# q turned as plain head pairs, q and k-v tiles in turn, and low parts of weights moved, in the projection of a hybrid encoder layer

## The chip, the cores and the metric

The kernel runs on one core of a Trainium2 chip. The metric is the device time of one execution in microseconds. TensorE (PE) multiplies and transposes, VectorE (DVE) and ScalarE (ACT) work element by element, GpSimd (POOL) does so more slowly, and SyncE (SP) issues the DMAs. Each engine works through its own list of instructions in order and waits on semaphores for what other engines make. PE writes into PSUM; DVE and ACT read it from there.

## The reference

One encoder layer over 1024 tokens of width 1024: a feed-forward half step, then attention and a state-space scan side by side on one input projection, an output projection, a second feed-forward half step and an embedding gate, each with a layer norm. What the change touches is the projection and what is done with q and k:

```python
u = x @ w_in[i]
q, k, v, z, xs, bm, cm, dt_raw = jnp.split(u, SPLIT_POINTS, axis=-1)
qf = _rms(q.reshape(B, S, N_Q_HEADS, HEAD_DIM), q_norm[i])
kf = _rms(k.reshape(B, S, N_KV_HEADS, HEAD_DIM), k_norm[i])
qh = _apply_rope(qf, cos, sin)
kh = _apply_rope(kf, cos, sin)
...
xbc = jnp.concatenate([xs, bm, cm], axis=-1)     # then a convolution over the tokens
```

There are 8 q heads and 2 k-v heads of 64.

## The kernel before

Everything is float32, and accuracy is kept by splitting each operand into a high part (rounded to the format that PE multiplies fast, made by a copy on ACT) and a low part (the rest, a subtraction `lo` on DVE, L87). `mm3` then makes three products for one: high by low, low by high, high by high (L122).

Tokens are cut into 8 tiles of 128. The stage in question is `qkv_part`. It stands between the products for z (with the layer norm of tokens 4 to 7 and their transposes, L224, beside them) and the eight tiles x0 to x7 of `xbc_part`, each of two halves of 512 tokens; a convolution over each x tile follows on ACT and DVE.

In `qkv_part` all eight q tiles (`qq`, 24 products of 128x512) come first, then all eight k-v tiles (`kv`, 24 products of 128x272). After each tile, `step` does three things with a lag. `norm` squares the tile on ACT (L865), sums it per head on DVE (L867) and takes the power -1/2 on GpSimd (L870). `rope` refines that with a Newton step and turns the pairs of q or k by the tables (L877 to L890). Then a `turn` transposes the result on PE: that of q transposes, for each of 8 heads, the 64 high and 64 low columns as one 128x128 block into a big PSUM buffer (L929), and ACT copies the 128x1024 result into Q (L930). To have them, q is split beforehand (a copy, L923, and a subtraction into `qs`). That of k transposes two blocks (L911) into a small buffer, and K's high and low parts are made from there (L913 and L87).

`step` takes one turn off the list `late` when more than `keep` wait there. The last turns are put on `self.pend` and taken by `pop`, two at a time, after each half of x0 (`xbc_gemm`). So x0's halves are each followed by two k turns.

PSUM has 2 big buffers of 128x1024 and 4 small ones of 128x512. x tiles use the big ones, and hold them until their convolution has read them.

Weights come by DMA into `raw` buffers, are cast by ACT into a ring of 10 blocks (L108), and their low parts are made by DVE. The k-v weights are loaded while the last two q tiles run (`kv_weights`), those of the x tiles (`wx`) when `xbc_weights` is called. A scheduler orders each engine's list by the order of the code and its dependences; `issue_after` and `behind` hold an instruction back behind a marked one.

Of the kernel before, what the change touches and what calls it, by code (L numbers as in the profile page):

```python
# [18 lines left out]
P = 128  # L19
# [17 lines left out]
class Layer:  # L37
# [771 lines left out]
        self.nc.sync.dma_start(out=t, in_=self.I[key].broadcast_to([P, n]))  # L809
        return t  # L810

    def kv_weights(self, part):
        if part == 0:
            self.wkv = []
        for k in ((0,), (3, 6))[part]:
            n = min(3, KD - k)
            r = self.raw(self.I["wkv"][:, k * 272:(k + n) * 272], n * 272)
            self.wkv += [self.split(r[:, i * 272:(i + 1) * 272], 272) for i in range(n)]
# [22 lines left out]
    def qkv_part(self, c, xT):  # L841
        nc, tc, I = self.nc, self.tc, self.I
        Q, K, V = self.qkv
        tabs = c.enter_context(tc.tile_pool(name="tabs", bufs=1))
        wk = c.enter_context(tc.tile_pool(name="qwork", bufs=2))
        cs = tabs.tile([P, NT, HD], F32, name="cs")
        sn = tabs.tile([P, NT, HD], F32, name="sn")
        nc.sync.dma_start(out=cs, in_=I["cs"])
        nc.sync.dma_start(out=sn, in_=I["sn"])
        dtb = self.bcast(tabs, "dtb", "dt_bias", 16)  # L850
        T = {}

        def tables(nm, scale):
            w = self.bcast(tabs, f"w_{nm}", f"{nm}n", HD)
            ws = self.bcast(tabs, f"ws_{nm}", f"{nm}ns", HD)
            T1 = tabs.tile([P, NT, HD], F32, name="T1")
            T2 = tabs.tile([P, NT, HD], F32, name="T2")
            for t_, a, b in ((T1, cs, w), (T2, sn, ws)):
                nc.vector.scalar_tensor_tensor(out=t_, in0=a, scalar=scale, in1=b.unsqueeze(1).broadcast_to([P, NT, HD]), op0=ALU.mult, op1=ALU.mult)
            T[nm] = (T1, T2)  # L860

        def norm(ps, nh):
            v = ps.rearrange("p (h d) -> p h d", d=HD)
            sq = wk.tile([P, nh, HD], F32, name="sq")
            nc.scalar.activation(out=sq, in_=v, func=AF.Square)  # L865
            ss = self.small.tile([P, 16], F32, name="ss")[:, :nh]
            nc.vector.reduce_sum(ss, sq, axis=AX.X)  # L867
            nc.vector.tensor_scalar(out=ss, in0=ss, scalar1=1.0 / HD, scalar2=RMS_EPS, op0=ALU.mult, op1=ALU.add)
            r = self.small.tile([P, 16], F32, name="qr")[:, :nh]
            nc.gpsimd.tensor_tensor(out=r, in0=ss, in1=self.mhalf[:, :nh], op=ALU.pow)  # L870
            return v, nh, sq, ss, r

        def rope(v, nh, m, ss, r, nm, t):

            self.newton(r, ss, nh)
            qn = wk.tile([P, nh, HD], F32, name="qn")
            nc.vector.tensor_tensor(out=qn, in0=v, in1=r.unsqueeze(2).broadcast_to([P, nh, HD]), op=ALU.mult)  # L877
            T1, T2 = (x[:, t] for x in T[nm])
            H2 = HD // 2
            for a in range(2):  # L880
                o = slice(a * H2, (a + 1) * H2)
                i = slice((1 - a) * H2, (2 - a) * H2)
                nc.vector.tensor_tensor(out=m[:, :, o], in0=qn[:, :, i], in1=T2[:, o].unsqueeze(1).broadcast_to([P, nh, H2]), op=ALU.mult)
            nc.vector.tensor_tensor(out=qn, in0=qn, in1=T1.unsqueeze(1).broadcast_to([P, nh, HD]), op=ALU.mult)
            if nm == "q":
                nc.vector.tensor_tensor(out=qn, in0=qn, in1=m, op=ALU.add)
                return qn
            kn = wk.tile([P, NKV, 2, HD], F32, name="kn", bufs=4)
            a, b = (x.unsqueeze(2).broadcast_to([P, NKV, 2, HD]) for x in (qn, m))
            nc.vector.tensor_tensor(out=kn, in0=a, in1=b, op=ALU.add)  # L890
            return kn

        NK = NKV * HD
        late = []

        def kv_front(t, ps):
            nc.vector.tensor_tensor(out=self.dt[:, t], in0=ps[:, 256:272], in1=dtb, op=ALU.add)
            vv = ps[:, NK:2 * NK].rearrange("p (g d) -> p g d", d=HD)
            st = norm(ps[:, :NK], NKV)
            nc.scalar.copy(out=V[:, t, :, 0], in_=vv)  # L900
            self.lo(V[:, t, :, 1], vv, V[:, t, :, 0])
            return st

        def kv_back(t, st):

            kn = rope(*st, "k", t)

            def turn():
                pt = self.pss()[:, :NKV * P].rearrange("p (g t) -> p g t", g=NKV)
                for g in range(NKV):  # L910
                    nc.tensor.transpose(out=pt[:, g], in_=kn[:, g].rearrange("p a d -> p (a d)"), identity=self.ident)  # L911
                hi, lo = (K[:, :, j, t * P:(t + 1) * P] for j in range(2))
                nc.scalar.copy(out=hi, in_=pt)  # L913
                self.lo(lo, pt, hi)
            late.append(turn)

        def q_front(t, ps):
            return norm(ps, NQ)

        def q_back(t, st):  # L920
            qs = wk.tile([P, NQ, 2, HD], F32R, name="qs", bufs=4)
            qn = rope(*st, "q", t)
            nc.scalar.copy(out=qs[:, :, 0], in_=qn)  # L923

            def turn():
                pt = self.psb().rearrange("p (h t) -> p h t", t=P)
                qv = qs.bitcast(F32)
                for hh in range(NQ):
                    nc.tensor.transpose(out=pt[:, hh], in_=qv[:, hh].rearrange("p a d -> p (a d)"), identity=self.ident)  # L929
                nc.scalar.copy(out=Q[:, :, t * P:(t + 1) * P], in_=pt)  # L930
            late.append(turn)
            return qs[:, :, 1], qn, qs[:, :, 0]

        backs, los = [], []

        def step(t, ps, front, back, keep=1):


            if len(late) > keep or not front:
                late.pop(0)()  # L940
            st = front(t, ps) if front else None
            if los:
                self.lo(*los.pop())
            if backs and (todo := backs.pop()()):
                los.append(todo)
            if front:
                backs.append(lambda: back(t, st))

        tables("q", HD ** -0.5)
        for t in range(NT):  # L950
            ps = self.qq(t, xT)
            if t >= NT - 2:
                self.kv_weights(t - NT + 2)
            step(t, ps, q_front, q_back)
        for t in range(NT):
            ps = self.kv(t, xT)
            step(t, ps, kv_front, kv_back, 2)
            if t == 0:
                tables("k", 1.0)
        self.pend += [lambda: step(NT, None, None, None)] * 4  # L960
        self.x0 = self.xbc_gemm(0, xT, 1)
        assert not late and not backs and not los

    def xbc_weights(self, j):
        return [b.rearrange("p l (k c) -> p l k c", c=P) for b in self.wload(self.I["wx"][j])]

    def xbc_half(self, w, xT, h, ps):
        self.mm3(ps, [((w[k // 4][:, 0, k % 4], w[k // 4][:, 1, k % 4]), tuple(x[:, k % 4] for x in xT[h][k // 4])) for k in range(KD)])
# [1 line left out]
    def xbc_gemm(self, j, xT, n):  # L970

        w = self.xbc_weights(j)
        ps = self.psb()
        for h in range(2):
            self.xbc_half(w, xT, h, ps[:, h * 512:(h + 1) * 512])
            if n == 1 or n and h:
                self.pop(2)
        return ps

    def xbc_part(self, c, wk, xT, prep):  # L980
# [18 lines left out]
        for j in range(8):  # L999
            a = wk.tile([P, S], F32, name="conv", bufs=3)  # L1000
            if j < 7:
                ps = self.x0 if j == 0 else self.xbc_gemm(j, xT, 2 if j > 1 else 0)
                conv(j, a, ps, 0, S, 0, S, True)
                nc.scalar.activation(out=a, in_=a, func=AF.Silu)
            else:
                w = self.xbc_weights(j)
                self.wz = [b for k in range(4) for b in self.wload(I["wz"][k])]
                p0, p1 = self.pss(), self.pss()
                self.xbc_half(w, xT, 0, p0)
                self.pop()  # L1010
# [1012 lines left out]
```

## Time and profile before

| | |
|---|---|
| median of 3 runs | 1939.07 us (1938.65 to 1939.66) |
| profiled execution | 1938.82 us, its span 1937.0 us |
| mean granted clock | 0.998 |
| stage q, k, v | PE from 696.8 us of the span, x1 from 784.4 |
| POOL busy, whole span | 418.2 us (22%) |

Times of lines are counted from the start of the span. The page of the profile gives each engine's busy time and the chain of work that ended last: followed back from the last instruction, at each step to what released it, or to the instruction before it on its engine. An engine with nearly all of that chain sets the time.

### The profile page before, as it was taken

Reading aid. Unit: us, or ns where it says so; the run is one execution under the profiler, and the core shown is the slowest. Engines: PE = TensorE matmul, PEld = TensorE weight load, DVE = VectorE, ACT = ScalarE, POOL = GpSimd, SP = SyncE. Lnnn points to the kernel's source line nnn. Section 1 sums busy time; section 2 is a strip of 40 time slices with the busy share of each in tenths; the row PEclk is TensorE's granted clock in tenths of the full one; section 3 lists DMA queues with packets and bytes.
Section 4 is the critical chain, followed back from the end, with each engine's and each line's share of the span. In section 5 each row is a group of like instructions: output and inputs, shape, how many; then the busy total and the mean of one; then the engine's idle time right before and its main releaser. Section 6 shows DMA issues by size and latency. Waiting matters only on the chain.

```text
span 1937.0 us, 25655 instructions
## 1 busy us (share of the span) xinstructions
PE 1926.7 (99%) x9130; PEld 1605.8 (83%) x9130; DVE 1524.2 (79%) x2362; ACT 877.5 (45%) x1502; POOL 418.2 (22%) x308
## 2 busy tenths in 40 slices
PE   9999999999999999999999999999999999999998
PEld 7888888888888889888888888888888888888886
DVE  7977777767678658758998888997787686877698
ACT  7433333334444224538897877633333333444311
POOL 0144544430001032001131001014444540001011
PEclk9999999999999999999999999999999999999999
DMA  8434554549866111241002663254544539976022
GB/s 307 134 127 156 189 186 147 196 155 392 279 218 219 61 44 47 88 126 63 6 1 90 218 211 126 92 173 144 184 177 165 188 118 358 333 261 224 27 78 97
DMA packets 147713, 310.34 MB, mean 160 GB/s; under 512 B 18128, under 2 KB 30800, under 8 KB 147584
## 3 DMA queue, kind: packets, MB, share of 16 engines
q1 hardware_dynamic: 147584, 308.69, 45.6%
q8 instruction: 72, 1.18, 0.3%
q14 instruction: 57, 0.47, 0.1%
HBM read 217.21 MB, written 91.42 MB: 159 GB/s over the span
## 4 chain that ended last, share of the span: by engine, by line
PE 99%; DVE 1%; DVEq 0%; issue 0%; ACT 0%
PE sm L122 56%; PE big L519 12%; PE sm L519 9%; PE big L122 6%; PE big L1192 3%; PE sm L1214 3%; PE sm L1229 2%; PE sm L1230 1%; PE sm L639 1%; PE sm L1410 1%; PE sm L1309 1%; PE sm L1320 1%; PE big L224 0%; PE big L929 0%; PE sm L224 0%; PE big L1725 0%
## 5 line engine op out<-in xcount | busy, mean ns | idle before, releaser
L122 PE MATMUL sm<-xh,blk 128*128 128x512 f32 x1424 | 439.8, 389 | 0.0
L122 PEld LDWEIGHTS sm<-xh,blk 128*128 128x128 f32 x1424 | 267.3, 188 | 55.3
L122 PE MATMUL sm<-xl,blk 128*128 128x512 f32 x736 | 283.8, 389 | 0.0
L122 PE MATMUL sm<-blk,xl 128*128 128x512 f32 (+2 forms) x704 | 208.1, 369 | 0.0
L108 ACT CAST blk<-raw 128x512 fp32r<-128x512 f32 (+1 forms) x168 | 101.1, 611 | 216.5 <-PE sm L122 135.3
L87 DVE TENSOR_TENSOR blk<-raw,blk 128x512 fp32r<-128x512 f32 (+1 forms) x168 | 141.6, 846 | 52.2 <-ACT blk L108 51.8
L108 ACT CAST blk<-s 128x512 fp32r<-128x512 f32 x172 | 105.7, 622 | 153.5 <-PE sm L122 126.0
L87 DVE TENSOR_TENSOR blk<-s,blk 128x512 fp32r<-128x512 f32 x176 | 141.8, 809 | 40.6 <-ACT blk L108 38.5
L178 POOL TENSOR_TENSOR ln_k<-ln_k,mhalf 128x1 f32<-128x1 f32 x32 | 37.8, 1185 | 578.2 <-DVE ln_k L177 562.0
L122 PEld LDWEIGHTS sm<-xl,blk 128*128 128x128 f32 x736 | 138.1, 188 | 28.8
L122 PE MATMUL sm<-blk,xh 128*128 128x512 f32 (+2 forms) x448 | 158.1, 373 | 0.0
L122 PEld LDWEIGHTS sm<-blk,xl 128*128 128x128 f32 x704 | 127.8, 188 | 20.8
L267 POOL TENSOR_TENSOR s<-raw 128x512 f32<-128x512 f32 x34 | 57.8, 1701 | 382.0 <-DVE blk L87 355.0
L519 PE MATMUL big<-xh 128*128 128x512 f32 x576 | 138.8, 390 | 0.0
L87 DVE TENSOR_TENSOR xh<-blk,xh 128x1024 fp32r<-128x1024 f32 x78 | 95.3, 1222 | 50.8 <-ACT xh L465 43.3
L465 ACT CAST xl<-blk 128x1024 fp32r<-128x1024 f32 x76 | 80.2, 1055 | 113.2 <-PE sm L519 45.1
L465 ACT CAST xh<-blk 128x1024 fp32r<-128x1024 f32 x78 | 82.2, 1054 | 107.1 <-PE big L519 45.4
L87 DVE TENSOR_TENSOR xl<-blk,xl 128x1024 fp32r<-128x1024 f32 x76 | 92.8, 1221 | 43.3 <-ACT xl L465 38.1
L519 PEld LDWEIGHTS big<-xh 128*128 128x128 f32 x576 | 107.8, 188 | 22.3
L519 PE MATMUL big<-xl 128*128 128x512 f32 x480 | 115.7, 390 | 0.0
L122 PE MATMUL sm<-xET2h,blk 128*128 128x512 f32 x352 | 108.3, 389 | 0.0
L122 PE MATMUL sm<-xET3h,blk 128*128 128x512 f32 x352 | 108.3, 389 | 0.0
(358 smaller groups left out, 4112.4 us busy)
## 6 DMA issues: line engine op xcount, KB each, us to landing
raw<-in_wi_dram SPq DMA_DIRECT2D x81, 512.0 KB
blk<-hS SPq DMA_DIRECT2D x154, 256.0 KB
hS<-h SPq DMA_DIRECT2D x88, 256.0 KB
wr<-in_wo_dram SPq DMA_DIRECT2D x44, 512.0 KB
blk<-wT SPq DMA_DIRECT2D x88, 256.0 KB
hS<-sg SPq DMA_DIRECT2D x66, 256.0 KB
wT<-wr SPq DMA_DIRECT2D x66, 256.0 KB
blk<-in_wo_dram SPq DMA_DIRECT2D x66, 256.0 KB
```

The source lines that it names most:

```text
L87: (eng or self.nc.vector).tensor_tensor(out=out, in0=full, in1=hi.bitcast(F32), op=ALU.subtract)
L108: self.nc.scalar.copy(out=b[:, 0, :n], in_=src)
L122: self.nc.tensor.matmul(ps, lhsT=a, rhs=b, start=(i == 0), stop=(i == n - 1))
L178: nc.gpsimd.tensor_tensor(out=r, in0=v, in1=self.mhalf[:, :1], op=ALU.pow)
L267: lambda: G.tensor_tensor(out=s1, in0=a21, in1=a22, op=ALU.add),
L465: A.copy(out=b[:, :, 0], in_=r)
L519: nc.tensor.matmul(ps[q], lhsT=b[:, 0, x, cut], rhs=b[:, 1, y], start=j == i == 0, stop=j == NP - 1 and i == 2)
L639: nc.tensor.matmul(o, lhsT=pT[t // 4][k][:, i, c], rhs=we[n][k][:, j], start=k + i + j == 0, stop=k + i == 2)
L1192: nc.tensor.matmul(ps[:, n * 512:(n + 1) * 512], lhsT=Q[:, h, q0:q0 + P], rhs=K[:, h // 4, j, n * 512:(n + 1) * 512], start=j == 0, stop=j ...
L1214: nc.tensor.transpose(out=pt[:, k], in_=pr[:, kk * P:(kk + 1) * P], identity=self.ident)
L1229: nc.tensor.matmul(po, lhsT=vw, rhs=pth[k // 4][:, k % 4], start=k == 0, stop=False)
L1230: nc.tensor.matmul(po, lhsT=vw, rhs=ptl[k // 4][:, k % 4], start=False, stop=k == KD - 1)
```

## The change

- q is not split before its turn. A turn now transposes the plain values of two heads as one 128x128 block, 4 blocks for 8 before. ACT copies the high parts from PSUM in two pieces of 64x512, DVE subtracts the low parts in two pieces of 64x512 into the other half of the partitions.
- The squares of q are eight instructions on ACT, one a head, that also sum; the sum on DVE falls away. k's stay as they were.
- q(t) and kv(t) alternate. The k-v weights are all loaded ahead of q(0), six of their blocks into buffers of their own. The tables for k are made in place by GpSimd.
- k's turns use a big buffer, except the last.
- The weights of x0 and x1 are loaded at the end of the loop. The low parts of the second block of x0's and of both of x1's are made by GpSimd. The loads of x2 and later are queued behind marks: behind DVE's last step of `qkv_part`, and behind the convolution of tile j-3.
- Of the last three turns, k6's comes after the first half of x0, those of q7 and k7 after the second.

```diff
 def norm(ps, nh):
+            if nh == NQ:
+                for h in range(nh):
+                    nc.scalar.activation(out=sq[:, h], in_=v[:, h], func=AF.Square, accum_out=ss[:, h:h + 1])
+            else:
+                nc.scalar.activation(out=sq, in_=v, func=AF.Square)
+                nc.vector.reduce_sum(ss, sq, axis=AX.X)
...
-                pt = self.pss()[:, :NKV * P].rearrange("p (g t) -> p g t", g=NKV)
+                pt = (self.psb if t < NT - 1 else self.pss)()[:, :NKV * P].rearrange("p (g t) -> p g t", g=NKV)
...
         def q_back(t, st):
-            qs = wk.tile([P, NQ, 2, HD], F32R, name="qs", bufs=4)
             qn = rope(*st, "q", t)
-            nc.scalar.copy(out=qs[:, :, 0], in_=qn)
 
             def turn():
-                pt = self.psb().rearrange("p (h t) -> p h t", t=P)
-                qv = qs.bitcast(F32)
-                for hh in range(NQ):
-                    nc.tensor.transpose(out=pt[:, hh], in_=qv[:, hh].rearrange("p a d -> p (a d)"), identity=self.ident)
-                nc.scalar.copy(out=Q[:, :, t * P:(t + 1) * P], in_=pt)
+                pt = self.psb()[:, :512].rearrange("p (h t) -> p h t", t=P)
+                for hp in range(NQ // 2):
+                    nc.tensor.transpose(out=pt[:, hp], in_=qn[:, 2 * hp:2 * hp + 2].rearrange("p h d -> p (h d)"), identity=self.ident)
+                both = [(slice(e * HD, (e + 1) * HD), slice((1 - e) * HD, (2 - e) * HD), Q[:, e::2, t * P:(t + 1) * P]) for e in range(2)]
+                for mine, other, q in both:
+                    nc.scalar.copy(out=q[mine], in_=pt[mine])
+                for mine, other, q in both:
+                    self.lo(q[other], pt[mine], q[mine])
...
+        for t_, nm in ((cs, "kn"), (sn, "kns")):
+            w = self.bcast(tabs, f"w_{nm}", nm, HD)
+            nc.gpsimd.tensor_tensor(out=t_, in0=t_, in1=w.unsqueeze(1).broadcast_to([P, NT, HD]), op=ALU.mult)
+        T["k"] = (cs, sn)
+        self.wx, self.wkv = [], []
+        for ks in ((0, 1, 2), (3, 4, 5), (6, 7)):
+            self.kv_weights(ks, kvp)
+        def wx(j):
+            r = self.raw(self.I["wx"][j])
+            with self.behind(mybir.EngineType.Activation), self.behind(mybir.EngineType.DVE):
+                self.wx.append([self.split(r[:, i * 512:(i + 1) * 512], eng=nc.gpsimd if j or i else None) for i in range(2)])
+
         for t in range(NT):
             ps = self.qq(t, xT)
-            if t >= NT - 2:
-                self.kv_weights(t - NT + 2)
+            if t == NT - 1:
+                wx(0)
             step(t, ps, q_front, q_back)
-        for t in range(NT):
-            ps = self.kv(t, xT)
-            step(t, ps, kv_front, kv_back, 2)
-            if t == 0:
-                tables("k", 1.0)
-        self.pend += [lambda: step(NT, None, None, None)] * 4
+            step(t, self.kv(t, xT), kv_front, kv_back)
+        wx(1)
+        self.pend += [lambda: step(NT, None, None, None)] * 3
...
+        self.marks = {2: self.last(mybir.EngineType.DVE)}
 
     def xbc_weights(self, j):
-        return [b.rearrange("p l (k c) -> p l k c", c=P) for b in self.wload(self.I["wx"][j])]
+        if j < len(self.wx):
+            blocks = self.wx[j]
+        else:
+            with self.tc.issue_after(self.marks[j]):
+                blocks = self.wload(self.I["wx"][j])
+        return [b.rearrange("p l (k c) -> p l k c", c=P) for b in blocks]
...
-                self.pop(2)
+                self.pop(2 if j or h else 1)
...
+                self.marks[j + 3] = self.last(mybir.EngineType.DVE)
```

How this moves instructions is shown at three places. The names carry buffer numbers here, so that one buffer can be told from another; the line numbers in rows of the change are its own.

**The start of x1.** On PE, before: the end of x0 (`big_6720`), the last two k turns in small buffers, and x1 (`big_6876`).

```order
L122 MATMUL big_6720<-xh10_5625,blk_6717 128x512
L122 MATMUL big_6720<-xl01_5624,blk_6717 128x512 x2
L911 MATMUL sm_6791<-ident_75,kn_6710 128x128 x2
L911 MATMUL sm_6796<-ident_75,kn_6760 128x128 x2
L122 MATMUL big_6876<-xh11_5366,blk_6870 128x512
L122 MATMUL big_6876<-xl10_5365,blk_6870 128x512 x2
```

On PE, after: the end of x0 (`big_6746`), the turns of q7 and k7, and x1 (`big_6894`).

```order
L122 MATMUL big_6746<-xh10_5625,blk_6650 128x512
L122 MATMUL big_6746<-xl01_5624,blk_6650 128x512 x2
L929 MATMUL big_6812<-ident_75,qn_6732 128x128 x4
L914 MATMUL sm_6821<-ident_75,kn_6786 128x128 x2
L122 MATMUL big_6894<-xh11_5366,blk_6740 128x512
L122 MATMUL big_6894<-xl10_5365,blk_6740 128x512 x2
```

Ahead of x1 there stands now a turn in a big buffer. On DVE, at the same place before: k's last rows, the steps for dt, the low parts of K, and the convolution of x0.

```order
L890 TENSOR_TENSOR kn_6760<-qn_6755,sq_6691 128x256
L87 TENSOR_TENSOR blk_7214<-raw_7212,blk_7214 128x512
L1100 TENSOR_SCALAR pm_6829<-dt_5821 128x128
L87 TENSOR_TENSOR blk_7217<-raw_7212,blk_7217 128x512
L1101 TENSOR_TENSOR pu_6830<-pm_6829,dt_5821 128x128
L87 TENSOR_TENSOR K_5819<-sm_6791,K_5819 128x2x128
L87 TENSOR_TENSOR K_5819<-sm_6796,K_5819 128x2x128
L1111 TENSOR_SCALAR pm_6829<-dt_5821 128x128
```

On DVE, after:

```order
L893 TENSOR_TENSOR kn_6786<-kr_6781,ksq_6718 128x256
L1119 TENSOR_SCALAR pm_6855<-dt_5821 128x128
L1120 TENSOR_TENSOR pu_6856<-pm_6855,dt_5821 128x128
L1130 TENSOR_SCALAR pm_6855<-dt_5821 128x128
L87 TENSOR_TENSOR Q_5820<-big_6812,Q_5820 64x4x128 x2
L87 TENSOR_TENSOR K_5819<-sm_6821,K_5819 128x2x128
L87 TENSOR_TENSOR blk_6953<-raw_6951,blk_6953 128x512
L87 TENSOR_TENSOR blk_6956<-raw_6951,blk_6956 128x512
```

q7's low parts stand behind the three dt steps, and the weights' low parts that stood among them have moved behind K.

**The low parts of q6.** On DVE, after, from the refinement of q7's power (`qr_6669`) to q7's end; `big_6708` is the buffer of q6's turn. Before, there is no low part made from q's turn.

```order
L129 TENSOR_TENSOR rs_t_6727<-qr_6669 128x8
L871 TENSOR_SCALAR ss_6719<-ss_6719 128x2
L130 TENSOR_TENSOR rs_t_6727<-rs_t_6727,ss_6659 128x8
L131 TENSOR_SCALAR rs_t_6727<-rs_t_6727 128x8
L132 TENSOR_TENSOR qr_6669<-qr_6669,rs_t_6727 128x8
L880 TENSOR_TENSOR qn_6732<-sm_6620,qr_6669 128x512
L886 TENSOR_TENSOR sq_6658<-qn_6732,T2_5842 128x8x32
L87 TENSOR_TENSOR Q_5820<-big_6708,Q_5820 64x4x128 x2
L886 TENSOR_TENSOR sq_6658<-qn_6732,T2_5842 128x8x32
```

q6's low parts stand in the middle of q7's rotation.

**Weights at the end of the loop.** On GpSimd, after: the powers of k6, q7 and k7 with the low parts of x0's second block (`blk_6650`) and of both of x1's (`blk_6740`, `blk_6743`). Before, this engine has powers alone here.

```order
L873 TENSOR_TENSOR qr_6605<-ss_6601,mhalf_76 128x2
L87 TENSOR_TENSOR blk_6650<-raw_6645,blk_6650 128x512
L873 TENSOR_TENSOR qr_6669<-ss_6659,mhalf_76 128x8
L87 TENSOR_TENSOR blk_6740<-raw_6738,blk_6740 128x512
L873 TENSOR_TENSOR qr_6723<-ss_6719,mhalf_76 128x2
L87 TENSOR_TENSOR blk_6743<-raw_6738,blk_6743 128x512
```

On ACT, after: the casts of x2's (`blk_6953`) and x3's weights (`blk_7075`), and the copies of the last turns.

```order
L932 CAST Q_5820<-big_6708 64x4x128 x2
L108 CAST blk_6953<-raw_6951 128x512
L108 CAST blk_6956<-raw_6951 128x512
L916 CAST K_5819<-big_6771 128x2x128
L108 CAST blk_7075<-raw_7073 128x512
L108 CAST blk_7078<-raw_7073 128x512
L932 CAST Q_5820<-big_6812 64x4x128 x2
L916 CAST K_5819<-sm_6821 128x2x128
```

The casts of x3's weights stand ahead of the copies of q7's turn.

More of the change, by code (lines that the diff above doesn't have):

```diff
@@ L810, in bcast, with kv_weights @@
         return t
[L812 to L818, printed above, removed]
+    def kv_weights(self, ks, pool):
+        r = self.raw(self.I["wkv"][:, ks[0] * 272:(ks[-1] + 1) * 272], len(ks) * 272)
+        for i, k in enumerate(ks):
+            b = pool.tile([P, 2, 272], F32R, name="wkv") if k < 6 else self.ring.tile([P, 2, 512], F32R, name="blk")
+            self.wkv.append(self.split_into(b, r[:, i * 272:(i + 1) * 272], 272))
     def kv(self, t, xT):
@@ L845, in qkv_part @@
         wk = c.enter_context(tc.tile_pool(name="qwork", bufs=2))
+        kvp = c.enter_context(tc.tile_pool(name="wkvp", bufs=6))
         cs = tabs.tile([P, NT, HD], F32, name="cs")
@@ L863, in norm @@
             v = ps.rearrange("p (h d) -> p h d", d=HD)
-            sq = wk.tile([P, nh, HD], F32, name="sq")
-            nc.scalar.activation(out=sq, in_=v, func=AF.Square)
+            sq = wk.tile([P, nh, HD], F32, name="sq" if nh == NQ else "ksq")
             ss = self.small.tile([P, 16], F32, name="ss")[:, :nh]
-            nc.vector.reduce_sum(ss, sq, axis=AX.X)
+            if nh == NQ:
[4 more added lines that the diff above has]
+                nc.vector.reduce_sum(ss, sq, axis=AX.X)
             nc.vector.tensor_scalar(out=ss, in0=ss, scalar1=1.0 / HD, scalar2=RMS_EPS, op0=ALU.mult, op1=ALU.add)
@@ L875, in rope @@
             self.newton(r, ss, nh)
-            qn = wk.tile([P, nh, HD], F32, name="qn")
+            qn = wk.tile([P, nh, HD], F32, name="qn", bufs=4) if nh == NQ else wk.tile([P, nh, HD], F32, name="kr", bufs=1)
             nc.vector.tensor_tensor(out=qn, in0=v, in1=r.unsqueeze(2).broadcast_to([P, nh, HD]), op=ALU.mult)
@@ L884, in rope @@
             nc.vector.tensor_tensor(out=qn, in0=qn, in1=T1.unsqueeze(1).broadcast_to([P, nh, HD]), op=ALU.mult)
-            if nm == "q":
+            if nh == NQ:
                 nc.vector.tensor_tensor(out=qn, in0=qn, in1=m, op=ALU.add)
                 return qn
-            kn = wk.tile([P, NKV, 2, HD], F32, name="kn", bufs=4)
+            kn = wk.tile([P, NKV, 2, HD], F32, name="kn")
             a, b = (x.unsqueeze(2).broadcast_to([P, NKV, 2, HD]) for x in (qn, m))
@@ L920, in q_back @@
         def q_back(t, st):
-            qs = wk.tile([P, NQ, 2, HD], F32R, name="qs", bufs=4)
             qn = rope(*st, "q", t)
-            nc.scalar.copy(out=qs[:, :, 0], in_=qn)
             def turn():
-                pt = self.psb().rearrange("p (h t) -> p h t", t=P)
-                qv = qs.bitcast(F32)
-                for hh in range(NQ):
-                    nc.tensor.transpose(out=pt[:, hh], in_=qv[:, hh].rearrange("p a d -> p (a d)"), identity=self.ident)
-                nc.scalar.copy(out=Q[:, :, t * P:(t + 1) * P], in_=pt)
+                pt = self.psb()[:, :512].rearrange("p (h t) -> p h t", t=P)
[6 more added lines that the diff above has]
+                    self.lo(q[other], pt[mine], q[mine])
             late.append(turn)
-            return qs[:, :, 1], qn, qs[:, :, 0]
         backs, los = [], []
         def step(t, ps, front, back, keep=1):
-            if len(late) > keep or not front:
+            if len(late) > keep or late and not front:
                 late.pop(0)()
```

## The prediction

> **What bounds the kernel now.** I read the page first: the busy times, then the chain that ended last.
>
> ```profile
> PE 1926.7 (99%) x9130; PEld 1605.8 (83%) x9130; DVE 1524.2 (79%) x2362; ACT 877.5 (45%) x1502; POOL 418.2 (22%) x308
> PE 99%; DVE 1%; DVEq 0%; issue 0%; ACT 0%
> ```
>
> TensorE (PE) is busy 1926.7 of 1937.0 us and makes up 99% of the chain. Then the busy times by stretch of 20 us over the stage that is changed (span, PE, PEld, DVE, ACT, POOL, granted clock).
>
> ```profile
> 710.00:730.00 20.00, 20.00 (x99) 16.70 (x97) 15.84 (x41) 6.32 (x9) 8.25 (x4) 1.00 0.00 0
> 750.00:770.00 20.00, 20.00 (x166) 20.00 (x165) 18.30 (x89) 6.83 (x19) 4.70 (x7) 1.00 0.07 27
> 770.00:790.00 20.00, 20.00 (x104) 16.98 (x103) 16.51 (x54) 10.55 (x23) 1.77 (x2) 1.00 0.47 143
> ```
>
> In the q tiles (first row), the k-v tiles (second) and around x0 (third) PE has no gap, at a clock of 1.00. So what the change takes from VectorE (DVE), ScalarE (ACT) or GpSimd (POOL) is worth nothing by itself. Only two things move the end: PE's own work, and any wait that PE has not got now. DVE is the nearest to becoming one, with 18.30 of 20 us in the k-v tiles.
>
> **What PE loses.** The timeline of PE gives start and duration. Since matmuls are pipelined, I price a turn from its start to the start of the next product.
>
> ```profile
> 718.68 1.04 PE L929 MATMUL big<-ident,qs 128*128 128x128 f32 x8
> 719.47 0.48 PE L122 MATMUL sm<-blk,xl 128*128 128x512 f32 x1
> ...
> 725.03 1.03 PE L929 MATMUL big<-ident,qs 128*128 128x128 f32 x8
> ...
> 759.56 0.37 PE L122 MATMUL sm<-blk,xl 128*128 128x272 f32 x1
> ...
> 762.65 0.38 PE L911 MATMUL sm<-ident,kn 128*128 128x128 f32 x2
> 762.79 0.37 PE L122 MATMUL sm<-blk,xl 128*128 128x272 f32 x1
> ...
> 778.10 0.60 PE L911 MATMUL sm<-ident,kn 128*128 128x128 f32 x4
> 778.46 0.47 PE L122 MATMUL big<-xh,blk 128*128 128x512 f32 x1
> ```
>
> Eight transposes cost 0.79 us (718.68 to 719.47), four 0.36, two 0.14; six are about 0.57 between these. A q tile's products take 5.56 (719.47 to 725.03), a k-v tile's 3.09. Before there are 8 turns of eight, 4 of two and 2 merged ones of four: 6.32 + 0.56 + 0.72 = 7.60. After, by the order: 7 of four, 7 of two, and q7 with k7 as one group of six: 2.52 + 0.98 + 0.57 = 4.07. There is one group more, and the first product behind a group is about 0.09 longer (0.48 against 0.39). **Term 1: -3.45 us.** That the transposed values are plain does not change a 128x128 transpose. This is all the change can give; 0.2% of the time, about what a measurement here can tell from no change, is 3.9 us.
>
> **A new wait at x1.** The rows of PE's order say x1 starts right behind the turns of q7 and k7. Those of DVE show both Q low parts right ahead of the work on x0. There are two big PSUM buffers: one is held by x0 until its convolution, the other takes q7's turn. So x1 cannot start before q7's turn is copied and both low parts are subtracted. Before, the turns ahead of x1 lay in the small buffers.
>
> ```profile
> 784.65 0.23 DVE L1100 TENSOR_SCALAR pm<-dt 128x128 f32<-128x128 f32 x1 [0.88 <-PE sm L911]
> 785.47 0.29 DVE L1101 TENSOR_TENSOR pu<-pm,dt 128x128 f32<-128x128 f32 x1
> ...
> 786.34 0.22 DVE L1111 TENSOR_SCALAR pm<-dt 128x128 f32<-128x128 f32 x1
> ...
> L1236 ACT COPY a_raw<-sm x16: 577/582/587, 900.1 to 1057.5; 64x512 f32<-64x512 f32 x16
> ...
> L1237 DVE TENSOR_TENSOR a_raw<-sm,a_raw x16: 672/690/696, 901.3 to 1058.2; 64x512 f32<-64x512 f32 x16
> ```
>
> The changed copies and low parts have no row of their own; attention's L1236 and L1237 have the same shape and source (64x512 from PSUM): 0.58 and 0.69. Count from the start S of q7's turn. k7's transposes end at S+0.70; pm, pu, pm (0.23, 0.29, 0.22) hold DVE to S+1.5. ACT's two copies end at about S+1.2 and S+1.75. The two low parts run S+1.5 to 2.2 and, overlapping by 0.08, to S+2.8. PE goes on at S+2.85 instead of S+0.57. **Term 2: +2.3 us.** Its lower end is 0 (another buffer is free after all), its upper 3.8, if ACT is late, as follows. In ACT's order the casts of wx(3) stand ahead of q7's copies, and their load starts once GpSimd has read wx(1).
>
> ```profile
> 772.54 0.33 SPq L94 DMA_DIRECT2D raw<-in_wx_dram  x1
> ...
> 775.90 1.14 ACT L108 CAST blk<-raw 128x512 fp32r<-128x512 f32 x2 [0.96 <-DMA raw<-in_wx_dram]
> ...
> L87 POOL TENSOR_TENSOR blk<-blk 128x512 fp32r<-128x512 f32 x8 | 10.4, 1297 | 33.1 <-ACT blk L108 33.1
> L267 POOL TENSOR_TENSOR s<-raw 128x512 f32<-128x512 f32 x34 | 57.8, 1701 | 382.0 <-DVE blk L87 355.0
> ```
>
> Issue to cast is 3.4 us, two casts 1.14, a GpSimd subtraction 1.3 to 1.7. Let E be the end of kv(7). GpSimd ends the power for q7 at E+2.8 (below), then wx(1) low part, power of k7 (0.75), second low part: E+6.1 to 6.9. The load lands by E+10.3, the casts end by E+11.5. The copies are wanted at E+12.4. That holds by about 1 us; a slow load would cost the other 1.5.
>
> **The loop of pairs.** A pair will be 0.36 + 5.56 + 0.14 + 3.09 = 9.15 us of PE.
>
> ```profile
> L930 ACT CAST Q<-big 128x1024 fp32r<-128x1024 f32 x8 | 8.1, 1018 | 4.1 <-PE big L929 4.1
> L870 POOL TENSOR_TENSOR qr<-ss,mhalf 128x8 f32<-128x8 f32 x8 | 16.9, 2117 | 29.9 <-DVE ss L868 29.9
> L877 DVE TENSOR_TENSOR qn<-sm,qr 128x512 f32<-128x512 f32 x8 | 5.5, 691 | 0.7
> L87 DVE TENSOR_TENSOR qs<-qn,qs 128x512 fp32r<-128x512 f32 x8 | 5.5, 688 | 2.1 <-ACT qs L923 2.1
> L867 DVE TENSOR_REDUCE ss<-sq 128x8 f32<-128x512 f32 x8 | 5.5, 684 | 4.3 <-ACT sq L865 4.2
> L865 ACT ACTIVATE sq<-sm 128x512 f32<-128x512 f32 x8 | 4.8, 599 | 21.1 <-PE sm L122 21.1
> L865 ACT ACTIVATE sq<-sm 128x128 f32<-128x128 f32 x8 | 2.2, 277 | 3.3 <-DVE kn L890 2.5 <-DVE rs_t L131 0.5
> L913 ACT CAST K<-sm 128x256 fp32r<-128x256 f32 x7 | 2.5, 370 | 6.5 <-PE sm L911 6.5
> ...
> L1201 ACT ACTIVATION_READ_ACCUMULATOR pr<-big,nm x64: 187/193/221, 877.1 to 1050.2; 128x1 f32 x64
> ```
>
> DVE: a q tile costs 15.84 x 6.35/20 = 5.0 now; a k-v tile 18.30 less the two tables at 0.685, 16.9 x 3.23/20 = 2.7. Take off the reduction (0.68) and the split (0.69), add two low parts (1.38): 7.7 of 9.15. GpSimd's power (2.1) can leave DVE idle for part of the 1.4 that remain, not for more. ACT: a square of 128x64 with its sum is not in the trace; the line through 0.60 and 0.28 gives 0.22, the read behind it 0.19, together 0.33 (overlapped) to 0.42, eight of them 2.7 to 3.4. With k's square, V, K (0.37) and two Q copies ACT has 4.8 to 5.5 of 9.15. The squares are the longer way now (3.4 against 0.60 + 0.68), and nobody waits for it: q(t)'s turn stands behind kv(t+1), 12.4 us after q(t) ends; squares and a K copy 3.7, the power 2.1, Newton 0.8, the four turns of the table 2.8, two Q low parts in between 1.4, hand-overs 0.3 make 11.1. **Term 3: 0**, with 1.3 us to spare.
>
> Less is left at the end of the loop. k6's turn takes the big buffer of q6's, 5.92 us after E, and must wait for q6's low parts; DVE has q7's rows ahead of them. q7's sum is ready at E-3.23+3.7+0.2 = E+0.7, the power ends E+2.8, Newton 3.6, first product 4.3, half of the next 4.7, two low parts 6.1. **Term 4: +0.2** (0 with squares at 0.33; +1.3 with a power of 3.2, the longest of eight).
>
> **What else moves.** The k-v weights are split ahead of the layer norm of tokens 4 to 7: eight low parts of 0.44, two of which stand there now, and two table products of 128x512 on GpSimd.
>
> ```profile
> L212 DVE SCALAR_TENSOR_TENSOR acc<-acc,ln_k,s x4: 1275/1284/1286, 668.4 to 685.6; 128x1024 f32<-128x1024 f32 x4
> ...
> L224 PE MATMUL big<-ident,acc x32: 270/273/273, 677.0 to 696.8; 128*128 128x128 f32 x32
> ```
>
> The first of these norms ends at 668.4 + 1.3 = 669.7, and PE turns it at 677.0: 7 us hide the six further low parts (2.6 on DVE), GpSimd's two products (2 x 1.7, ahead of the norms' powers) or a load that comes 3 late. wx(0)'s low part on GpSimd stands ahead of q7's power, so it is done by E+0.7, and x0 reaches that half at E+3.1; wx(1)'s second is done by E+6.9, and x1 starts behind E+12. Those queued later (wx(2) behind the last DVE step of the stage, wx(j+3) behind conv(j)) have a tile of 11 us (two halves of 5.56) ahead of them. Cost 0, and 1 to 3 if one load comes late.
>
> **Sum.** -3.45 + 2.3 + 0 + 0.2 = -0.95. The profiled execution took 1938.82 (span 1937.0 and 1.8 around it), so 1937.87; the median of the three runs is 0.25 above it: **1938.1**.
>
> **A rule against it.** While GpSimd made this power, DVE ran the two-input split beside it.
>
> ```profile
> 727.38 2.06 POOL L870 TENSOR_TENSOR qr<-ss,mhalf 128x8 f32<-128x8 f32 x1 [4.24 <-DVE ss L868]
> ...
> 728.63 0.69 DVE L87 TENSOR_TENSOR qs<-qn,qs 128x512 fp32r<-128x512 f32 x1 [0.69 <-ACT qs L923]
> ```
>
> The split took its usual 0.69 inside a power of 2.06, so DVE was not held up; by these rows GpSimd's low parts cost DVE nothing. The Trainium skill, "SBUF — State Buffer", Who interferes with whom, says the pair of ports that VectorE and GpSimd share is an exclusive lock, held for a whole instruction, also against VectorE operations with two SBUF inputs. By that rule three low parts of 1.3 to 1.7 on GpSimd would hold such DVE steps ahead of x1, up to 4.5 us, and the trace's two rows speak against it here; rival C has the same price.
>
> **Rivals.**
> A. No wait at x1: only -3.45 + 0.2 or less, 1935.6 to 1935.8. For it: the copies are short. Against: the order has the low parts behind three steps and x1 needs that buffer. Chance 0.14.
> B. The q turns of four cost as much as those of eight, so the change does not save what it says: 7 x 0.43 = +3.0, 1941.1. Against: 0.36 at 778.10. Chance 0.04.
> C. GpSimd or ACT come late at the end (powers of 3.2, the load of wx(3), DVE held up during three GpSimd subtractions): +1.5 to 4.5 on top, 1939.6 to 1942.6. Chance 0.13.
> D. Slower: DVE becomes the bound of the pairs. It decides where DVE's work and its waits for the power pass 9.15 us a pair: once the 1.3 us to spare are used, every pair pays. At 10.1 a pair it is 8 x 0.95 - 1.3 = +6.3, so 1944.4. For it: 18.30 of 20 now, and powers that alternate for q and k. Against: 7.7 of 9.15. Chance 0.08.
> E. A slow clock behind the gap: the trace shows 1.00 in every stretch, and no gap of PE in this stage, so it cannot show what 2.3 us idle do. If half clock followed for 3.4 us, as long as a load takes, about 1.7 us are added: 1939.8. Chance 0.03. The Trainium skill, "TensorE: Matmul & The Clock Gate", Part 1, has the clock halved after an idle window of about 3.4 us; a gap of 2.3 is below it, one of 3.8 is not.
>
> **How the numbers follow.** The forecast, 1937.2 to 1939.3 with the bounds of terms 2 and 4, has 0.58. Range: 1935.4 to 1941.3 takes in A, B, E and the near half of C; D and the rest of C are left out. Faster by over 0.2% (below 1935.2) only as A's edge, 0.03; slower (above 1942.9) is D and an edge of C, 0.09; within, 0.88.
>
> **What would show it.** PE's timeline of the changed kernel: turns of four at 0.36; no gap at the q turns of the pairs; one gap of about 2.3 us ahead of x1, released by DVE's low part of Q; at most a short one at k6's turn. DVE at about 17 of 20 us within the pairs; the granted clock 1.00 behind x1. I am wrong if gaps stand at every q turn (D), if x1 follows at once (A), or if the clock drops (E).

## The result, and the profile after

| | median | range | ratio to before |
|---|---|---|---|
| before | 1938.89 us (22 runs) | 1938.08 to 1940.08 | |
| the change | 1941.31 us (22 runs) | 1939.82 to 1943.55 | 1.0013 (1.0008 to 1.0019) |

The change is slower by 2.4 us. Forecast were 0.95 us less. It is within 0.2%, as was thought likely, but on the other side, and just past the end of the range (1941.3).

The page of the changed kernel, busy times and chain:

```profile
PE 1924.3 (99%) x9098; PEld 1602.4 (83%) x9098; DVE 1530.2 (79%) x2357; ACT 881.2 (45%) x1622; POOL 422.7 (22%) x313
PE 97%; DVE 1%; issue 0%; DMA 0%; ACT 0%; POOL 0%; DVEq 0%; SPq 0%; ACTq 0%; POOLq 0%
```

PE does 32 transposes less and is 2.4 us less busy, in a span that is 1.9 longer: it waits now. The view of the waits lists PE's (engine, line, what it waited for, us, times, longest). In the kernel before, this view has only the one at the start, L634.

```profile
PE big L122 <- ACT conv L1010: 2.6, 1, 2.6
PE big L634 <- DVE s L631: 1.2, 1, 1.2
PE big L914 <- DVE Q L87: 0.8, 1, 0.8
PE sm L1328 <- DVE state L1345: 0.8, 1, 0.8
```

PE's timeline of the changed kernel around the first q turn, the turn of k6, and the turns of q7 and k7 with the start of x1:

```profile
713.49 0.60 PE L929 MATMUL big<-ident,qn 128*128 128x128 f32 x4
713.84 0.48 PE L122 MATMUL sm<-blk,xl 128*128 128x512 f32 x1
...
773.92 0.61 PE L122 MATMUL big<-xl,blk 128*128 128x512 f32 x2
775.36 0.41 PE L914 MATMUL big<-ident,kn 128*128 128x128 f32 x2 [0.82 <-DVE Q L87]
...
781.09 0.60 PE L929 MATMUL big<-ident,qn 128*128 128x128 f32 x4
781.53 0.38 PE L914 MATMUL sm<-ident,kn 128*128 128x128 f32 x2
784.47 0.47 PE L122 MATMUL big<-xh,blk 128*128 128x512 f32 x1 [2.56 <-ACT conv L1010]
```

A q turn costs 0.35 us, as forecast. k6's turn stands 1.44 behind two products that take 0.46 steadily: a wait of 1.0. x1 starts 2.94 behind a turn of 0.14: a wait of 2.8. (The row names ACT's step for x0 because it ended last; the order of the code, and the runs below, give q7's low parts.) The starts of q(0) and x1 give the sum of the stage; before:

```profile
696.82 0.48 PE L122 MATMUL sm<-blk,xl 128*128 128x512 f32 x1
...
784.37 0.48 PE L122 MATMUL big<-xh,blk 128*128 128x512 f32 x1
```

and after, beside the 784.47 above:

```profile
696.45 0.48 PE L122 MATMUL sm<-blk,xl 128*128 128x512 f32 x1
```

The stage takes 87.55 us before and 88.02 after. Without the two waits of 3.8 it would be 84.2: PE's own work became 3.3 shorter, where 3.45 were forecast. So in this execution 0.5 of the loss lies in the stage. The starts of the same products, beside those of the kernel before, show the rest: the change is 0.4 earlier from the first 30 us on, 0.1 later at x1, 0.3 later at 1096 us, 1.5 later at 1109 and 1.9 at the end. So 1.2 arise from 1096 to 1109 us, in the state scan, which the change does not touch. And the runs differ among themselves, as the experiments show next.

**Why q6's low parts were late.** DVE and GpSimd of the changed kernel, timelines of the same stretch, behind the row of PE that follows kv(7) (the E of the prediction):

```profile
768.45 0.60 PE L929 MATMUL big<-ident,qn 128*128 128x128 f32 x4
...
770.33 1.27 DVE L130 TENSOR_TENSOR rs_t<-rs_t,ss 128x8 f32<-128x8 f32 x1
...
772.76 1.05 DVE L886 TENSOR_TENSOR sq<-qn,T 128x256 f32<-128x256 f32 x1
773.82 1.39 DVE L87 TENSOR_TENSOR Q<-big,Q 64x512 fp32r<-64x512 f32 x2
...
768.43 1.66 POOL L873 TENSOR_TENSOR qr<-ss,mhalf 128x8 f32<-128x8 f32 x1 [4.62 <-DVE ss L871]
770.27 1.31 POOL L87 TENSOR_TENSOR blk<-raw,blk 128x512 fp32r<-128x512 f32 x1 [0.17 <-ACT blk L108]
...
772.20 1.32 POOL L87 TENSOR_TENSOR blk<-raw,blk 128x512 fp32r<-128x512 f32 x1
```

A DVE product of 128x8, 0.17 elsewhere, lasts 1.27 and ends at 771.60, with GpSimd's subtraction (771.58). One of 128x256, 0.42 elsewhere, ends at 773.81, 0.3 after the second. Both read two operands in SBUF. Together they come 1.7 late, and the low parts, which end at 775.21, release k6's turn. That is 6.8 us after E, where 6.1 were worked out. But the power for q7 ran from E to E+1.6, where E+0.7 to E+2.8 were allowed: without the 1.7 the low parts would have ended at about E+5.0, and k6's turn, wanted at E+5.9, would not have waited at all.

**Why x1's wait is 2.8 and not 2.3.** The last of the three dt steps on DVE, ACT's two copies of q7 and DVE's two low parts, which start only behind both copies:

```profile
782.54 0.23 DVE L1130 TENSOR_SCALAR pm<-dt 128x128 f32<-128x128 f32 x1
...
781.73 1.17 ACT L932 CAST Q<-big 64x512 fp32r<-64x512 f32 x2 [3.54 <-PE big L929]
...
782.93 1.39 DVE L87 TENSOR_TENSOR Q<-big,Q 64x512 fp32r<-64x512 f32 x2 [0.17 <-ACT Q L932]
```

From the start S of q7's turn (781.09), the low parts were worked out from S+1.5, behind the first copy, to S+2.8. The dt steps end at S+1.7 and the second copy at S+1.8; the low parts run from there to S+3.2, and x1 starts 0.15 later.

### The profile page after: what moved, and what is told of

Its sections match the earlier page's. It is cut to its first block, busy times and chain, and to the rows that moved or that the text cites. A ratio compares the mean times of both kernels' runs of the same rounds, so it can differ in the third digit from the quotient of the medians.

```text
span 1938.9 us, 25713 instructions
## 1 busy us (share of the span) xinstructions
PE 1924.3 (99%) x9098; PEld 1602.4 (83%) x9098; DVE 1530.2 (79%) x2357; ACT 881.2 (45%) x1622; POOL 422.7 (22%) x313
## 4 chain that ended last, share of the span: by engine, by line
PE 97%; DVE 1%; issue 0%; DMA 0%; ACT 0%; POOL 0%; DVEq 0%; SPq 0%; ACTq 0%; POOLq 0%
PE sm L122 56%; PE big L519 12%; PE sm L519 9%; PE big L122 6%; PE big L1211 3%; PE sm L1233 3%; PE sm L1248 2%; PE sm L1249 1%; PE sm L639 1%; PE sm L1429 1%; PE sm L1328 1%; PE sm L1339 1%; PE big L224 0%; PE big L1744 0%; PE sm L224 0%
## 5 line engine op out<-in xcount | busy, mean ns | idle before, releaser
L122 PE MATMUL sm<-blk,xl 128*128 128x512 f32 (+1 forms) x608 | 190.3, 381 | 0.0
L122 PE MATMUL sm<-blk,xh 128*128 128x512 f32 (+2 forms) x400 | 144.1, 383 | 0.0
L122 PEld LDWEIGHTS sm<-blk,xl 128*128 128x128 f32 x608 | 112.7, 188 | 20.8
```

The costliest lines, as they stand in the source:

```text
L122: self.nc.tensor.matmul(ps, lhsT=a, rhs=b, start=(i == 0), stop=(i == n - 1))
```

## The experiments

All are compared with the kernel before, run beside them. The theory at the start: the change gains 3.3 us on PE and pays two waits for big PSUM buffers, one made by GpSimd.

**The change again, for a second trace.**

> The change as it is, for a second trace. Theory A (two waits that are in the code): ratio to before 1.001 to 1.002 again; PE waits about 1.0 us ahead of k6's turn and 2.8 us ahead of x1, and the 1.3 us lost in the state scan near 1095 to 1105 us of the span are chance, so they differ from the first trace by more than 0.5 us. Theory B (the loss in the scan belongs to the change): it stands at the same place with 1.0 to 1.5 us again.

1941.81 us, ratio 1.0014 (1.0005 to 1.0023). The waits at k6 and x1 are the same, 0.95 and 2.8. The scan's wait is there again, with 1.2, so it was not chance. And this execution shows what the first trace did not. PE's timeline behind x1's start, then the windows (span, PE, PEld, DVE, ACT, POOL, granted clock):

```profile
785.12 0.49 PE L122 MATMUL big<-xh,blk 128*128 128x512 f32 x1 [2.56 <-ACT conv L1010]
785.42 1.03 PE L122 MATMUL big<-xl,blk 128*128 128x512 f32 x2
786.26 0.63 PE L122 MATMUL big<-xh,blk 128*128 128x512 f32 x1
...
776.00:780.00 4.00, 3.99 (x19) 3.33 (x20) 3.71 (x13) 1.51 (x3) 0.00 (x0) 1.00 0.23 89
782.02:785.44 3.42, 0.86 (x7) 0.61 (x6) 2.56 (x7) 3.01 (x5) 0.00 (x0) 1.00 0.28 59
785.44:788.85 3.41, 3.41 (x10) 2.63 (x9) 3.41 (x5) 1.33 (x3) 0.00 (x0) 0.50 0.30 95
789.00:793.00 4.00, 4.00 (x19) 3.25 (x19) 4.00 (x6) 1.57 (x3) 0.00 (x0) 1.00 0.09 35
```

For 3.4 us behind the gap the clock is 0.50 and a product takes 0.43 instead of 0.23: 8 x 0.2 = 1.6 us lost. All 33 runs of the change part by their mean clock: the 12 with 0.999 took 1939.8 to 1940.8, the 21 with 0.998 or less 1941.0 to 1943.6, 1.4 us more in the median. So the slow stretch is taken to be in those 21, though only this trace of the two shows one. Before, runs of 0.998 and 0.999 do not differ that way (1938.5 and 1938.8).

**The two buffers.** Once q7's turn alone, then k6's too, takes a small buffer:

```diff
-                pt = self.psb()[:, :512].rearrange("p (h t) -> p h t", t=P)
+                pt = (self.psb if t < NT - 1 else self.pss)()[:, :512].rearrange("p (h t) -> p h t", t=P)
...
-                pt = (self.psb if t < NT - 1 else self.pss)()[:, :NKV * P].rearrange("p (g t) -> p g t", g=NKV)
+                pt = (self.psb if t < NT - 2 else self.pss)()[:, :NKV * P].rearrange("p (g t) -> p g t", g=NKV)
```

> q7's turn in a small PSUM buffer, so that x1's big buffer is free. Theory A: no wait at x1, the k6 wait of 1.0 us stays: 2.8 us less than the change, so about 1938.5 where the change has 1941.3 and before 1938.9; ratio to before 0.9990 to 1.0000. Rival (the wait only moves, to k7's turn, to x2 or to the scan): within 0.7 us of the change.

> q7's and k6's turns both in small PSUM buffers. Theory A: neither wait, 3.8 us less than the change: about 1937.5 in the median where losses behind the stage stay, 1935.6 where they go with the gap; ratio to before 0.998 to 0.9995. Rival (the waits move): over 1939.

1938.57 us, ratio 1.0000 (0.9991 to 1.0008), and 1937.40 us, 0.9995 (0.9986 to 1.0003). Each wait goes with its buffer, and no stretch of half clock is left. In place of x1's wait comes a smaller one; PE's waits with both buffers, beside the one at the start:

```profile
PE sm L1171 <- ACT ldt L1137: 1.0, 1, 1.0
PE sm L1328 <- DVE state L1345: 0.5, 1, 0.5
```

x1 being earlier, DVE has taken its convolution ahead of the dt steps, and ldt comes late. The theory holds; a part of the rival too.

**GpSimd.** The low parts of x0's and x1's weights all on DVE:

```diff
-                self.wx.append([self.split(r[:, i * 512:(i + 1) * 512], eng=nc.gpsimd if j or i else None) for i in range(2)])
+                self.wx.append([self.split(r[:, i * 512:(i + 1) * 512]) for i in range(2)])
```

> The change with the low parts of x0's and x1's weights on VectorE instead of GpSimd. Theory L (GpSimd's subtraction holds up VectorE steps with two SBUF inputs for its whole length, 1.1 and 0.6 us in the rows ahead of q6's low parts): the k6 wait goes, no VectorE step of 128x8 lasts over 0.3 us there, the x1 wait of 2.8 us stays; 1.0 us less than the change. Rival (VectorE is simply late at the end of the loop): three more subtractions of 0.69 on it make the k6 wait longer, 1.0 to 2.5 us, and the time 0 to 1.5 us above the change.

1940.82 us, ratio 1.0009 (1.0000 to 1.0018), 1.0 us less than the change beside it. k6's wait is gone, x1's is 2.95. The same product on DVE, and q6's low parts:

```profile
769.89 0.19 DVE L130 TENSOR_TENSOR rs_t<-rs_t,ss 128x8 f32<-128x8 f32 x1
...
771.49 1.39 DVE L87 TENSOR_TENSOR Q<-big,Q 64x512 fp32r<-64x512 f32 x2
```

It takes 0.19 again. DVE was not late by its own work: with more to do it is earlier. (The scheduler also put x1's low parts behind q6's here, at 775.05.)

**No wait left in the stage.** Both small buffers, and the convolution of x1 queued behind the dt steps:

```diff
-                conv(j, a, ps, 0, S, 0, S, True)
+                with (self.tc.issue_after(self.dt_mark) if j == 1 else ExitStack()):
+                    conv(j, a, ps, 0, S, 0, S, True)
...
+            if j == 0:
+                self.dt_mark = self.last(mybir.EngineType.DVE)
```

> q7's and k6's turns in small buffers, and the convolution of x1 queued behind the dt steps on VectorE, so that the wait of 1.0 us for ldt at 805 us, which showed when the two waits were gone, goes too. Theory A (the time is PE's own work plus its waits): 1.0 us less than with the two buffers alone (1937.4): 1936.4, ratio to before 0.998 to 0.9992, granted clock 0.999 in all runs. Rival (VectorE passes the delay on to x3): 1937 to 1938.5.

1936.66 us, ratio 0.9990 (0.9981 to 0.9998). ldt's wait is gone; only the scan's is left (1.1 in its trace). The granted clock was not 0.999 in all runs, as expected, but 0.998 in some; their times are not the longer ones, and the trace has no slow stretch.

**A longer gap.** The change with q7's low parts made twice (the second pair writes the same values):

```diff
-                for mine, other, q in both:
+                for mine, other, q in both + both * (t == NT - 1):
                     self.lo(q[other], pt[mine], q[mine])
```

> The change with q7's two low parts made twice, so that the gap ahead of x1 grows by 1.4 us from 2.8 to 4.2. Theory C (a gap of this length sometimes lets the clock fall to half for some 3 us, more often the longer it is): the mean granted clock is 0.998 or less in nearly all runs (12 of 22 with the change), and the median rises by more than the 1.4 us, to 1943.5 to 1945 where the change has 1941.3. Rival (the clock is no part of it): 1.4 us more, 1942.7, with a spread like the change's.

1945.80 us in the median of 5 runs (1945.67 to 1946.18), ratio 1.0037 (1.0024 to 1.0049), all with a clock of 0.997. The gap grew by more than meant, to 5.9 us (x1 starts at 787.5), since the scheduler put the second pair behind the weights' low parts. The windows behind it:

```profile
788.00:792.70 4.70, 4.70 (x12) 3.63 (x11) 4.70 (x7) 1.14 (x2) 0.00 (x0) 0.50 0.15 62
793.00:797.00 4.00, 4.00 (x19) 3.30 (x18) 3.74 (x11) 2.35 (x2) 0.00 (x0) 1.00 0.27 85
```

Against the undisturbed runs of the change (1940.4) that is 5.4 more. The half clock stands from 786.0, still within the gap, to 792.8: 3.1 of gap and half of the 5.3 behind x1's start make 5.7. So the clock is part of it, and by the mean clock it fell in all five runs.

The traces also show why it falls in one run of the change and not in another. In every trace the clock changes only at whole steps of 3.41 us, counted from where it first rises at the start: it falls 778.24 us after that in the second trace of the change and with the low parts on DVE, 781.65 here and with the squares as before (below), 761.17 with the plain turn alone (next). These are 228, 229 and 223 steps, and the slow stretch lasts one step or two. Windows laid on such steps, in the first trace of the change, with the low parts on DVE, and with the plain turn alone:

```profile
779.61:783.02 3.41, 2.30 (x14) 1.74 (x12) 0.83 (x4) 1.25 (x3) 0.00 (x0) 1.00 0.00 0
783.02:786.44 3.42, 1.97 (x9) 1.65 (x10) 3.38 (x6) 3.08 (x5) 0.00 (x0) 1.00 0.27 60
...
779.52:782.93 3.41, 1.38 (x10) 0.97 (x8) 1.59 (x5) 3.06 (x6) 0.00 (x0) 1.00 0.10 14
782.93:786.34 3.41, 2.73 (x7) 2.19 (x8) 3.38 (x6) 2.31 (x4) 0.00 (x0) 0.50 0.21 63
...
756.85:760.26 3.41, 1.73 (x13) 1.30 (x12) 3.35 (x11) 0.91 (x3) 0.00 (x0) 1.00 0.02 5
763.67:767.08 3.41, 1.56 (x11) 1.23 (x11) 3.24 (x19) 0.92 (x4) 1.04 (x2) 1.00 0.00 0
767.08:770.50 3.42, 3.42 (x18) 3.42 (x17) 2.10 (x11) 0.43 (x2) 0.39 (x1) 0.50 0.00 0
```

What tells one step from another in these traces is PE's idle time within it. Behind a step at full clock with 1.85 us idle or more (1.85, 2.03, 2.56 twice, 3.41) the next one stood at 0.50; behind one with 1.68 or less it did not. In the first trace of the change a border between steps, at 783.02, parts the gap ahead of x1 into 1.11 and 1.45, and the clock stays; in the second the gap lies in one step (782.02 to 785.44, 2.56 idle). So whether a gap of this size costs the half clock is a matter of where the border falls.

**The plain turn alone**, in the kernel before: `q_back` as in the change, all the rest as it was (the last turns k's).

> Of the change only the turn of plain head pairs (four transposes, two copies and two low parts of 64x512), put into the kernel before: all q tiles first, then all k-v tiles, the last turns k's in small buffers. Theory A: 8 x 0.43 = 3.4 us less than before and no new wait at x1, so 1935.2 to 1935.6. Rival (VectorE becomes the bound of the q tiles, 5.7 us of work and the wait for the power in 5.92): waits at the q turns of 0.2 to 0.8 us each, 1936.5 to 1941.

1944.79 us, ratio 1.0029 (1.0018 to 1.0040): the rival, and worse. PE's largest waits of this kernel in the stage, then its windows in the q tiles and where the k-v tiles begin:

```profile
PE sm L122 <- DVE qn L877: 2.0, 1, 2.0
PE big L926 <- DVE qn L886: 1.2, 1, 1.2
PE sm L122 <- DVE K L87: 1.1, 1, 1.1
...
730.00:750.00 20.00, 20.00 (x123) 17.80 (x122) 18.10 (x47) 9.14 (x19) 3.90 (x4) 1.00 0.21 68
746.00:766.00 20.00, 14.27 (x109) 13.14 (x107) 19.22 (x61) 6.46 (x18) 4.14 (x4) 1.00 0.15 52
```

The q tiles still hold, at 18.1 of 20 on DVE. Where k-v tiles, with half the work on PE, meet the low parts of the last q, DVE has 19.22 of 20 and PE waits 5.7 of 20 us. No wait is over 2.0 us, yet two of them fall into one step and bring the half clock from 767.1 to 770.5 (the last two rows of the windows above), another 1.7 us. In the change the plain turn has no such waits. There the tiles alternate, and the tables and the loads of weights have moved as well; which of these is needed was not tested one by one.

**Squares as before**: one square on ACT and the sum on DVE, in the change.

> The change with q's squares as before: one square of 128x512 on ScalarE and the sum over heads on VectorE. Theory A (eight squares with their sums take ScalarE 0.2 us each, and VectorE has 1.5 to 2 us a pair to spare, so this part decides nothing in the loop): no gap at the q turns; VectorE is 0.6 us a pair busier, and the wait at k6's turn grows by 0 to 0.7 us: 0 to 1 us above the change. Rival (VectorE is at its limit without this part): gaps of 0.3 us or more at several q turns, 2 to 6 us above the change.

1942.59 us, ratio 1.0017 (1.0008 to 1.0027), 0.8 above the change run earlier. No gap at the q turns; k6's wait is 1.9, 0.9 more, a little past what was expected. In the loop this part decides nothing; at its end it is worth a microsecond.

**The wait in the scan.** In the changed kernel, and in every one so far with fewer transposes, a DVE step in the scan waits longer for a write of y to land. Timelines of the change (SP's issue, then DVE):

```profile
1097.05 0.34 SPq L1431 DMA_DIRECT2D yd<-y  x1
...
1100.49 0.69 DVE L1419 TENSOR_TENSOR y<-xb,dsk 128x512 f32<-128x512 f32 x1 [2.23 <-DMA yd<-y]
```

and of the kernel before:

```profile
1096.84 0.34 SPq L1412 DMA_DIRECT2D yd<-y  x1
...
1098.94 0.69 DVE L1400 TENSOR_TENSOR y<-xb,dsk 128x512 f32<-128x512 f32 x1 [1.03 <-DMA yd<-y]
```

3.4 us from issue to use against 2.1. The view of the DMAs by queue, in the 1.5 us behind the issue in the change, has one packet that is not there before:

```profile
q1 hardware_dynamic: 165, 0.32, 54.1%
q8 instruction: 1, 0.02, 5.1%
```

It is a fetch of instructions of 16 KB. Before, the packet in this part of the scan runs at 1092.4, alone. The 72 packets of this queue match PE's some 18,300 instructions, 256 each, and the change takes 32 products and 32 weight loads off PE's list, a quarter of a packet. So all later fetches come later in the program, this one into the write. Two kernels move it, by tiny matmuls in the warm-up at the start, of whose 14 full ones 7 stay. In the first, the kernel without waits gets 32 matmuls more; in the second, the kernel before gets 96, three quarters of a packet. The edit of the first:

```diff
-        for i in range(14):
-            nc.tensor.matmul(o, lhsT=zero[:, :P], rhs=zero[:, :512], start=True, stop=True)
+        for i in range(46):
+            m, n = (P, 512) if i >= 39 else (2, 32)
+            nc.tensor.matmul(o[:m, :n], lhsT=zero[:, :m], rhs=zero[:, :n], start=True, stop=True)
```

> The kernel without the waits, with 32 more matmuls in PE's warm-up at the start (39 tiny ones and 7 full, for 14 full), so that PE's instruction stream has its old length. Theory F (the change took 64 instructions off PE's stream, so the 16 KB fetch of its instructions, at 1092.4 us in the kernel before, now falls into the write of y at 1097 us, holds one DMA queue for 1 us and makes VectorE and then PE wait for the state): the fetch stands 4 to 6 us ahead of that write again, y's write lands 2.1 us after its issue instead of 3.5 to 3.8, and PE's wait of 1.1 us is gone: 1.1 us less than 1936.7, so 1935.6 (up to 1936.3 if the warm-up starts the first products 0.5 us later). Rival (the wait belongs to the order of the work): the wait of 0.4 to 1.2 us stays, 1936.7.

> The kernel before with 96 more tiny matmuls in the warm-up (192 instructions, three quarters of a fetch of 256), so that PE's fetches stand as in the change. Theory F: the fetch falls into the write of y, which lands 3 to 3.8 us after its issue instead of 2.1, and a wait of PE for the state of 0.4 to 1.3 us appears in the scan, which neither trace of the kernel before has. Rival: no such wait. The start may be 1 to 4 us later, so the time says nothing here.

The first: 1936.03 us, ratio 0.9985 (0.9976 to 0.9994), 0.6 less than the kernel without waits, and PE's wait for the state is gone. (Expected were 1.1 less; with the other warm-up, PE's products from 60 us on start 0.6 later than in that kernel.) y's write, issued at 1093.53, lets DVE go on at 1095.62. The second, with one run of 1941.68 us, shows the wait in a kernel whose work behind the warm-up is that of before; PE's wait, and DVE's:

```profile
PE sm L1310 <- DVE state L1327: 0.9, 1, 0.9
...
1101.79 0.69 DVE L1401 TENSOR_TENSOR y<-xb,dsk 128x512 f32<-128x512 f32 x1 [2.35 <-DMA yd<-y]
```

with the packet on the instruction queue inside the write again. One more look at the kernel before as it is had no wait there:

> The kernel before, for a second trace. Theory S (a wait of 0.4 to 1.2 us for the state in the scan, L1328 of the changed kernel, belongs to the change): no such wait here, as in the first trace. Rival (it is chance in either kernel, from the landing of the y writes): it may stand here too, with 0.3 to 1.2 us.

1938.98 us, and the same 2.1 us from issue to use. So the wait belongs to the change, and comes through the length of PE's list. The traces agree: beside the kernel before, PE loses 0.9 to 1.7 us between 1096 and 1109 us in all nine with the shorter list and the old warm-up and in the second of the two kernels above, and nothing in the first and in the kernel before itself.

## Why the prediction was wrong

- **The bound** was right: PE's list and its waits set the time, and what the other engines gained was worth nothing by itself.
- **Term 1** (-3.45) measured -3.3: right.
- **Term 2** (x1 waits for q7's low parts) was the right mechanism at the right place, sized 2.3 and measured 2.8. DVE starts the low parts 0.3 later than was worked out, behind longer dt steps and behind both copies instead of the first; the low parts and the step on to PE take 0.2 more.
- **Term 3** (0) held: no gap at a q turn. A square with its sum takes 0.2 a head, under the bounds of 0.33 to 0.42.
- **Term 4** (+0.2 at k6's turn) measured +1.0, and the sum failed here first. The place and the chain were right. The durations in it were 1.1 too long (the power began 0.7 earlier and took 1.66 instead of 2.1) and would by themselves have left no wait; that the term is not off by more is luck. What it left out is what the rule on the shared ports said and the prediction set aside. The row chosen against the rule was a power on GpSimd, beside which DVE ran at its usual 0.69. A subtraction of 128x512 on GpSimd is the operation that was added, and beside it DVE steps with two SBUF operands stood still, 1.7 us in all. By the rule of the Trainium skill ("SBUF — State Buffer", Who interferes with whom) that was to be expected; the trace agrees for the subtraction, with 1.27 for 0.17, and not for the power.
- **The clock** (rival E, chance 0.03) came in 21 of 33 runs, by their mean clock. The forecast relied on a gap of 2.3 us being below an idle window of 3.4; a gap of 2.8 is also below it, and the clock still fell. In the traces 1.85 us idle within one step were enough, so the gap that was forecast could have brought it too. The price that the rival named, 1.7, is what it cost (1.6). The Trainium skill ("TensorE: Matmul & The Clock Gate", Part 1) has the idle window at about 3.4 us and free-running. The steps of 3.41 in the traces agree with both; the idle time needed to bring it on is less here, 1.85 of 3.41.
- **The fetch of instructions** was not thought of. It cost 1.2 in the profiled execution.

Together, in the profiled execution: -3.3 + 1.0 + 2.8 + 1.2 = +1.7, where its span is 1.9 longer; the start is 0.4 earlier and small steps behind the stage add 0.6, for which no cause was sought. The median of all runs lies above that one since more than half of them pay the clock too.

The gain was there. Taking the waits away one by one gives a kernel 2.75 us faster than before (1936.03 and 1938.78, with the other warm-up); the interval of its ratio, 0.9976 to 0.9994, leaves out 1.

## What to carry to other kernels

When PE has no gap, a change that saves work elsewhere can only cost: list every buffer that PE will have to wait for at the new place, and give the last turns buffers that the next products do not need. Count PE's idle time within any stretch of 3.4 us, in one gap or in several, and where it comes to half of that add the price of the half clock behind it, 1.7 us here. Before moving work to GpSimd, see which DVE steps with two SBUF operands run beside it, and compare with a row of the same operation.

## What the runs showed of the hardware

- A GpSimd subtraction of 128x512 (1.31 us) held a DVE product of 128x8 with two SBUF operands until it ended (1.27 for 0.17), while a GpSimd power of 128x8 (2.06) did not hold a DVE subtraction (0.69).
- TensorE's clock changed only at steps of 3.41 us. Behind a step with 1.85 us or more of PE's time idle (five traces) it stood at 0.50 for one step or two; behind one with 1.68 or less it stayed at 1.00. A gap of 2.8 us brought this in more than half of the runs, by their mean clock, and one of 5.9 in all five.
- PE's instructions are fetched in packets of 16 KB that take about 1 us on one DMA queue. Where one falls into a transfer for which an engine waits, that lands over 1 us later, so that taking instructions off PE's list can cost time 300 us behind.
